# Edge keys of a windowed attention: the high and the low part of the weights on the two halves of the rows, in two products in place of four

## The chip, the cores and the metric

The kernel runs on one core of a Trainium2 chip. The metric is the device time of one execution in microseconds. A core has five engines with queues of their own: TensorE (PE in the profile, its weight loads PEld), VectorE (DVE), ScalarE (ACT), GpSimd (POOL) and SyncE (SP), which here issues most of the DMAs. Each queue is worked off in order; semaphores hold an instruction until what it reads is there.

## The reference

One layer of an encoder, applied to two requests of 2048 tokens with shared weights, all in float32. What the change touches is the first of two attentions, group A: a windowed attention with 8 query heads, 2 key-value heads and head width 64.

```python
def block(j):                                   # 128 queries, 384 keys: 128 before, the block, 128 after
    sc = jnp.einsum('bqkgd,bskd->bkgqs', qb, kb) * scale
    valid = band & ((kpos >= 0) & (kpos < s))   # |key - query| <= 128
    sc = jnp.where(valid, sc, -jnp.inf)
    m = jnp.maximum(jnp.max(sc, axis=-1, keepdims=True), sink_f)
    e = jnp.exp(sc - m)
    denom = jnp.sum(e, axis=-1, keepdims=True) + jnp.exp(sink_f - m)
    o = jnp.einsum('bkgqs,bskd->bqkgd', e / denom, vb)
...
o_a = windowed_gqa_sink(q_a, k_a, v_a, sink_a) * jax.nn.silu(g_a)
o_b = neighbourhood_attn(q_b, k_b, v_b, rpb_b) * jax.nn.silu(g_b)
x = x + jnp.concatenate([o_a, o_b], axis=-1) @ w_out
return x + (p @ w_ple) * jax.nn.sigmoid(x @ w_ple_gate)
```

Before it stand an RMS norm, one combined input projection, a norm of queries and keys and a partial rotary embedding; after it a second attention (group B) and the output layers.

## The kernel before, in words

**Two parts for each number.** TensorE multiplies in a format that keeps fewer bits than float32 (float32r). So an operand is kept as a high part (the value rounded to float32r) and a low part (the rest), and a product of two operands is a sum of products of parts. The values v of the first attention lie in a tile `vv`, rows = 128 keys, and for each key-value head 128 columns: 64 of the high part beside 64 of the low part. One product with that as the stationary operand gives both, in two halves of the rows of the result.

**Units.** The first attention goes over 32 blocks of 128 queries (`f` = 0 to 31, 16 of each request; `t` is the block in its request), each in two units, one for each key-value head (`kv`), so 64 units. A unit has 4 query heads. Its queries are split into two halves of 64, and for each half only the 320 keys that its window can reach are scored: with respect to the block, the first half needs keys -128 to 191, the second -64 to 255. Of the softmax weights, turned so that keys are rows (`pt`, line 775), there are thus three groups of rows:

- the edge keys, `pt(0)`: 64 rows. For the first half of the queries these are the first 64 keys of the next block (called right here), for the second half the last 64 keys of the block before (left). Each has 256 columns: 4 heads x 64 queries.
- `pt(1)`: 128 rows, keys of the block before for the first half of the queries and of the next for the second, 256 columns each;
- `pt(2)`: 128 rows, the block's own keys, 512 columns.

The weights come out of PSUM into three tiles `p_rot[0..2]` of 128 rows x 2 x 512 columns, which live for the whole first attention: ScalarE writes the high part (line 797, index 0 of the middle dimension), VectorE the low part (line 799, index 1). The edge keys' tile is `p_rot[0]`: the right side's weights lie in rows 0 to 63 of columns 0 to 255, the left side's in rows 64 to 127 of columns 256 to 511. The other half of the rows of each is zero, written once by two memsets of GpSimd (lines 791 and 792).

**The products.** `po(j)` (line 802) multiplies values with weights into one PSUM tile. `po(0)`: for each side that there is, two products of 256 columns, one with the high part and one with the low part of the weights, so four in an inner block and two in a block at an end of its request. The stationary operand is the neighbour block's whole value tile of 128 rows; the zeroed rows keep the other 64 keys out. `po(1)`: four products of 256 columns; `po(2)`: two of 512 columns. All products are recorded at line 287 (in `mm`), those of the weights under the name `po<-pr,vv`. `fin` (line 813) adds the two halves of the rows of the result and multiplies with the gate.

**The order of the work.** TensorE's order is written out by hand: each product is tied to the one before it (`pinned`). Between a unit's steps a stream of projection products (`pk`, `pq`, `pg`) of the block two ahead is given out by their costs, and a plan (`PLAN_A`, line 93) says at which share of the unit's stretch which step comes: (share, 1 for this unit and 0 for the one before, step, index). So scores (`sc`) of a unit stand in its own stretch, and its `pt`, `po` and `fin` in the next one's; the first head's `po(0)` thus comes in the second head's stretch at 0.48. The other engines' order comes from the compiler's scheduling, except where an instruction is tied to its place by `P` or `behind`.

**DMAs around it.** `turn` (line 749) copies a unit's softmax weights onto themselves in another format, 2 DMAs of 320 KB from SP (line 753, `tna<-s`); `pt` transposes them in the next stretch. `turn_gate` (line 366) and `turn_q` (line 740) do the same for gates and queries. Line 399 loads inputs, line 827 stores results. The projection's values are written into `vv` at lines 573 and 574, a block ahead of the block that uses them as its right neighbour.

Of the kernel before, what the change touches and what calls it, by code (L numbers as in the profile page):

```python
# [11 lines left out]
F32 = mybir.dt.float32  # L12
F32R = mybir.dt.float32r
AF = mybir.ActivationFunctionType
ALU = mybir.AluOpType
# [4 lines left out]
NT = SEQ // 128  # L20
# [38 lines left out]
def bias_offsets():  # L59
# [33 lines left out]
PLAN_A = (  # L93
    (0.04, 1, "sc", 0), (0.08, 1, "sc", 1), (0.11, 1, "sc", 2), (0.12, 1, "rest", 0), (0.14, 1, "sc", 3),
    (0.14, 1, "rest", 1), (0.21, 0, "pt", 0), (0.26, 0, "pt", 1), (0.30, 1, "qcopy", 0), (0.31, 0, "pt", 2),
    (0.32, 1, "exp", 0), (0.33, 1, "turn", 0), (0.33, 1, "turn", 1),
    (0.48, 0, "po", 0), (0.56, 0, "po", 1), (0.64, 1, "prep", 0), (0.66, 0, "po", 2), (0.67, 1, "den", 0), (0.74, 0, "fin", 0),
    (0.75, 1, "gcopy", 0),
)
# [25 lines left out]
def emit(ctx, tc, io):  # L125
    nc = tc.nc
# [4 lines left out]
    def ptile(shape, tag, name):  # L131
        tag = PSM.get(tag, tag)
        return pp.tile(shape, F32, tag=tag, name=name, bufs=PSB[tag])

    main = ctx.enter_context(tc.tile_pool(name="main", bufs=1))
# [136 lines left out]
    def pinned(ins):  # L272

        if last_pe:
            tc.add_manual_dep(ins.ins, last_pe.pop().name,
                              mybir.DependencyInfo(mybir.DependencyClass.NoSync, mybir.DependencyReason.DATA),
                              reason="tensor engine order")
        last_pe.append(ins.ins)
# [7 lines left out]
    def mm(out, lhsT, rhs, start, stop):  # L286
        pinned(nc.tensor.matmul(out, lhsT, rhs, start=start, stop=stop))  # L287
# [22 lines left out]
    def sm_tiles():  # L310
        return {"s": [], **{k: ap.tile([128, 4], F32, tag=k, name=k, bufs=3) for k in ("mx", "nm", "den", "rd")}}
# [51 lines left out]
    def turn_gate(sm):  # L363

        g2r = ap.tile([128, 256], F32R, tag="g2r", name="g2r", bufs=1)
        nc.sync.dma_start(g2r.bitcast(F32), sm["g2"])
        sm["g2"] = g2r
# [15 lines left out]
    ap = ab_stack.enter_context(tc.tile_pool(name="ab", bufs=1))  # L383
# [55 lines left out]
    def big(shape, dt, name):  # L439
        return ap.tile(shape, dt, tag="big", name=name, bufs=3)  # L440
# [69 lines left out]
    for i in range(4):  # L510
        nc.vector.tensor_tensor(out=tab[i // 2][:, i % 2], in0=cs[:, i % 2],
                                in1=rw[:, i].unsqueeze(1).broadcast_to([128, NT, 16]), op=ALU.mult)
# [7 lines left out]
    vv = big([128, NT, 2, 2, HD], F32R, "vv")  # L520
    q2s = []
    for i in range(2):
        t = ap.tile([128, 2, 512], F32R, tag=f"q2{i}", name=f"q2{i}")
# [205 lines left out]
    p_rot, s2, tn, tna, turned_q = [], [0], [], [], {}  # L729

    def turned_a():

        if not tna:
            tna.append(ap.tile([128, 1920], F32R, tag="ev", name="tna", bufs=1))
        return tna[0]

    def turn_q(f):

        turned_q[f] = turned_a()[:, 1280:1792].rearrange("p (h d) -> p h d", d=HD)
        nc.sync.dma_start(turned_q[f].bitcast(F32), held[f][0])  # L740

    def unit_a(f, kv):
        s, t = divmod(f, NT)
        _, gs, y = held[f]
        left, right = t > 0, t < NT - 1
        span = [(0 if left else 128 - 64 * half, 320 if right else 256 - 64 * half) for half in range(2)]
        sm, pairs, prs, got = sm_tiles(), [], [], {}

        def turn(pair):

            if left and right:
                to = turned_a()[:, 640 * pair:640 * pair + 640]
                nc.sync.dma_start(to.bitcast(F32), pairs[pair])
                pairs[pair] = to

        def sc(i):
            pair, half = divmod(i, 2)
            a, z = span[half]
            c0, n = 128 * t - 128 + 64 * half, z - a
            if half == 0:  # L760
                k = 640 * (s2[0] % 4)
                pairs.append(space[:, k:k + 640])
                s2[0] += 1
                if not right:
                    nc.gpsimd.memset(pairs[pair][:, 256:320], 0.0)
            ps = ptile([128, 512], "sc", "sc")
            for j, q in enumerate(qs[f]):
                mm(ps[:, :n], q[kv][:, 128 * i:128 * i + 128], ks_a[:, kv, c0 + a:c0 + z], j == 0, j == 1)
            softmax(i, ps, n, mask[:, a:z], sm, pairs[pair][:, 320 * half + a:320 * half + z])
            if i == 3:  # L770
                got["ex"] = exps(sm, y[:, 11:12], gs[:, 256 * kv:256 * kv + 256],
                                 (snk[:, 0, 4 * kv:4 * kv + 4], snk[:, 1, 4 * kv:4 * kv + 4]))
                next(got["ex"])

        def pt(j):
            pt = ptile([128, 512], "pt", "pt")
            r, c = slice(0, 128), slice(0, 512)
            if j == 0:
                r, c = slice(0 if right else 64, 128 if left else 64), slice(0, 256)
                for pair in range(2):  # L780
                    tr(pt[:r.stop, 128 * pair:128 * pair + 128], pairs[pair][:, 256:256 + r.stop])
            else:
                if j == 1:
                    c = slice(0 if left else 256, 512 if right else 256)
                for x in range(c.start // 128, c.stop // 128):
                    half, pair = divmod(x, 2)
                    col = ((0, 512), (128, 384))[j - 1][half]
                    tr(pt[:, 128 * x:128 * x + 128], pairs[pair][:, col:col + 128])
            if not p_rot:
                p_rot.extend(main.tile([128, 2, 512], F32R, tag="p_t", name="pr", bufs=3) for _ in range(3))  # L790
                nc.gpsimd.memset(p_rot[0][64:128, :, 0:256].bitcast(F32), 0.0)
                nc.gpsimd.memset(p_rot[0][0:64, :, 256:512].bitcast(F32), 0.0)
            pr = p_rot[j]
            parts = [(r, c, c)] if j else \
                [(slice(64 * x, 64 * x + 64), c, slice(256 * x, 256 * x + 256)) for x, there in enumerate((right, left)) if there]
            for r, c, to in parts:
                nc.scalar.copy(pr[r, 0, to], pt[r, c])  # L797
            for r, c, to in parts:
                nc.vector.tensor_tensor(out=pr[r, 1, to], in0=pt[r, c], in1=pr[r, 0, to].bitcast(F32), op=ALU.subtract)
            prs.append(pr)  # L800

        def po(j):
            if j == 0:
                got["po"] = ptile([128, 512], "ms", "po")
            first, second = slice(0, 256), slice(256, 512)
            steps = ([(1, first)] * right + [(-1, second)] * left, [(-1, first)] * left + [(1, second)] * right,
                     [(0, slice(0, 512))])[j]
            for d, c in steps:
                v = vv[:, t + d, kv].rearrange("p a d -> p (a d)")
                for i in range(2):  # L810
                    mm(got["po"][:, c], v, prs[j][:, i, c], j == 0 and i == 0 and d == steps[0][0], j == 2 and i == 1)

        def fin(_):
            pgt = ptile([128, 2, 128], "sc", "pgt")
            for i in range(2):
                tr(pgt[:, i, :], sm["g2"][:, 128 * i:128 * i + 128])
            ot = ap.tile([128, 2, 128], F32, tag="ot", name="ot", bufs=2)
            ph2 = got["po"].rearrange("p (x i e q) -> p e x i q", x=2, i=2, e=2)
            oh = ot.rearrange("p i (x q) -> p x i q", x=2)
            for e in range(2):  # L820
                a, z = 64 * e, 64 - 64 * e
                nc.scalar.copy(oh[a:a + 64], ph2[z:z + 64, e])
            for e in range(2):
                a = 64 * e
                nc.vector.tensor_tensor(out=oh[a:a + 64], in0=ph2[a:a + 64, e], in1=oh[a:a + 64], op=ALU.add)
            nc.vector.tensor_tensor(out=ot, in0=pgt, in1=ot, op=ALU.mult)
            nc.sync.dma_start(oa_d[s].rearrange("(i p) q -> p i q", p=128)[:, 2 * kv:2 * kv + 2, 128 * t:128 * t + 128],
                              ot)
        return {"sc": sc, "turn": turn, "gcopy": lambda _: turn_gate(sm) if f < 2 * NT - 2 else None,
                "qcopy": lambda _: turn_q(f + 1) if kv == 0 and f + 1 < 2 * NT - 2 else None, "pt": pt, "po": po, "fin": fin, "prep": lambda _: nxt(f) if kv else None,  # L830
                "exp": lambda _: next(got["ex"]), "den": lambda _: next(got["ex"]), "rest": lambda _: None if kv else next(qrest[f])}

# [345 lines left out]
    first = [filler(0), filler(1)]  # L1178
# [83 lines left out]
    with tc.tile_pool(name="c", bufs=1, reuse_waits="tile") as op:  # L1262
# [208 lines left out]
        for m in range(7 * len(groups)):  # L1471
            n, i = divmod(m, 7)
# [94 lines left out]
```

## Time and profile before

| | |
|---|---|
| median of 3 runs | 2429.82 us (2428.88 to 2432.13) |
| the profiled execution | 2431.07 us |
| its span, first to last instruction | 2429.3 us |
| granted TensorE clock, mean | 1.000 |
| product groups `po<-pr,vv` of 256 columns | 480 |
| of 512 columns | 128 |

How to read it: the profile is of one execution, a little above the median of the runs; the span leaves out what lies around the first and the last instruction. A row of a group names line, engine, operation, tile written <- tiles read, shape written <- shape read, xcount, then busy time in us, mean ns of one, and idle time of the engine just before them with what ended it. A row of the timeline has the start in us, the length in us from the first one's start to the last one's end, and how many instructions were merged (x4). TensorE's products are pipelined, so that one starts before the one ahead has ended; the step from start to start is what one takes of the queue. "idle before <- DVE pr L799" says that the engine sat idle until VectorE had written `pr` at line 799.

### The profile page before, as it was taken

The page shows a single profiled execution, that of the slowest core. Times are in us where ns is not written, and L with a number is a line of the kernel's source. Part 1 is how long each engine was busy: PE and PEld are TensorE (multiplying, and loading weights), DVE is VectorE, ACT ScalarE, POOL GpSimd, SP SyncE. Part 2 cuts the span into 40 slices and gives each one's busy share as a digit, 9 for nine tenths or more (in the row PEclk, how much of TensorE's full clock was granted, in tenths as well). Part 3 has the DMA queues.
Part 4 walks back from the last instruction along what each step waited for, and adds up shares of the span by engine and source line. Part 5 has one row for each costly group of instructions (what it writes and reads, how often), then busy time and mean ns, then how long its engine had stood idle before and what let it go on. Part 6 is the DMA issues. An engine that isn't in the chain of part 4 may idle for free.

```text
span 2429.3 us, 41554 instructions
## 1 busy us (share of the span) xinstructions
PE 2417.4 (100%) x13062; PEld 2047.4 (84%) x13062; DVE 1729.2 (71%) x4215; ACT 1427.6 (59%) x3408; POOL 848.3 (35%) x1363
## 2 busy tenths in 40 slices
PE   9999999999999999999999999999999999999999
PEld 7888888888888888888888888888888888888887
DVE  7888888888875666666666667776537665776876
ACT  6777777777764656665566666666753122344433
POOL 5555555555543544444455444443100000000000
PEclk9999999999999999999999999999999999999999
DMA  6655554555574677668876777788976545856765
GB/s 229 210 185 183 185 179 146 178 183 185 187 243 149 207 245 259 233 212 260 279 237 229 234 256 251 245 267 263 323 274 233 165 161 186 270 177 207 247 225 170
DMA packets 304204, 531.87 MB, mean 219 GB/s; under 512 B 34384, under 2 KB 126960, under 8 KB 299760
## 3 DMA queue, kind: packets, MB, share of 16 engines
q1 hardware_dynamic: 274320, 490.02, 60.3%
q10 hardware_dynamic: 29664, 39.19, 5.3%
q8 instruction: 104, 1.70, 0.3%
q14 instruction: 116, 0.95, 0.1%
HBM read 307.72 MB, written 134.23 MB: 182 GB/s over the span
## 4 chain that ended last, share of the span: by engine, by line
PE 94%; DMA 2%; ACT 1%; DVE 1%; issue 1%; POOL 0%; SPq 0%; ACTq 0%; DVEq 0%
PE pvg L287 15%; PE pqk L287 15%; PE acca L1370 14%; PE accc L1370 10%; PE pg L287 7%; PE pq L287 7%; PE scb L287 4%; PE pk L287 3%; PE po L287 3%; PE pob L287 3%; PE sc L287 3%; PE pple L287 3%; PE ptb L291 2%; PE pt L291 2%; PE ptb L293 1%
## 5 line engine op out<-in xcount | busy, mean ns | idle before, releaser
L287 PE MATMUL pvg<-wb,xr 128*128 128x512 f32 x1536 | 471.3, 408 | 0.3 <-DVE rd L354 0.3
L287 PE MATMUL pqk<-wa,xr 128*128 128x512 f32 x1536 | 432.3, 408 | 0.0
L331 ACT ACTIVATE s<-s,nm 128x320 f32<-128x320 f32 (+6 forms) x512 | 294.6, 579 | 44.3 <-DVE nm L324 30.0
L287 PEld LDWEIGHTS pvg<-wb,xr 128*128 128x128 f32 x1536 | 273.4, 189 | 33.1 <-DMA wb<-sp_1wb 0.8
L287 PEld LDWEIGHTS pqk<-wa,xr 128*128 128x128 f32 x1536 | 265.1, 188 | 38.9
L1352 ACT CAST opd<-raw 128x512 fp32r<-128x512 f32 x224 | 131.5, 618 | 269.4 <-PE acca L1370 116.6
L417 POOL TENSOR_TENSOR xr<-stx,xr 128x512 fp32r<-128x512 f32 x186 | 238.0, 1295 | 104.3 <-ACT xr L416 78.7
L1353 DVE TENSOR_TENSOR opd<-raw,opd 128x512 fp32r<-128x512 f32 x224 | 146.5, 685 | 145.4 <-ACT opd L1352 145.4
L287 PE MATMUL pq<-wa,xr 128*128 128x512 f32 x768 | 240.8, 405 | 0.0
L287 PE MATMUL pg<-wb,xr 128*128 128x512 f32 x768 | 229.5, 405 | 0.4 <-DVE vv L574 0.4
L306 DVE CUSTOM_DVE_ANT_0 s<-scb,bias 128x288 f32<-128x288 f32 (+3 forms) x256 | 139.1, 548 | 73.9 <-PE scb L287 47.2
L1052 ACT COPY otb<-pob 64x512 f32<-64x512 f32 x128 | 74.3, 581 | 182.4 <-PE pob L287 181.8
L1370 PE MATMUL accc<-opd,wb 128*128 128x512 f32 x768 | 176.7, 389 | 0.0
L1370 PE MATMUL acca<-opd,wa 128*128 128x512 f32 (+1 forms) x780 | 175.9, 386 | 0.5 <-ACT r L1448 0.5
L1370 PE MATMUL acca<-opd,s 128*128 128x512 f32 x768 | 175.4, 389 | 0.0
L1370 PEld LDWEIGHTS acca<-opd,wa 128*128 128x128 f32 x780 | 145.0, 188 | 30.2 <-ACT r L1448 0.7
L1370 PEld LDWEIGHTS accc<-opd,wb 128*128 128x128 f32 x768 | 144.2, 188 | 29.9
L1370 PEld LDWEIGHTS acca<-opd,s 128*128 128x128 f32 x768 | 144.2, 188 | 29.9
L170 POOL TENSOR_TENSOR yb<-vrb,power 128x8 f32<-128x8 f32 x64 | 106.2, 1659 | 152.3 <-DVE vrb L872 134.6
L287 PEld LDWEIGHTS pg<-wb,xr 128*128 128x128 f32 x768 | 135.7, 188 | 16.8 <-DVE vv L574 0.8
L797 ACT CAST pr<-pt 128x512 fp32r<-128x512 f32 (+2 forms) x248 | 112.1, 474 | 54.3 <-PE pt L291 47.3
L287 PEld LDWEIGHTS pq<-wa,xr 128*128 128x128 f32 x768 | 132.7, 189 | 11.3
(196 smaller groups left out, 5143.3 us busy)
## 6 DMA issues: line engine op xcount, KB each, us to landing
tna<-s SPq DMA_DIRECT2D x112, 320.0 KB
stx<-x_b SPq DMA_DIRECT2D x128, 256.0 KB
vw<-v_d SPq DMA_DIRECT2D x96, 256.0 KB
v_d<-vb SPq DMA_DIRECT2D x64, 256.0 KB
xres<-x_r SPq DMA_DIRECT2D x64, 256.0 KB
raw<-x_d SPq DMA_DIRECT2D x16, 1024.0 KB
xres<-ple_d SPq DMA_DIRECT2D x64, 256.0 KB
xres<-x_d SPq DMA_DIRECT2D x64, 256.0 KB
```

The lines of the kernel that those rows point to most:

```text
L170: nc.gpsimd.tensor_tensor(out=y, in0=v, in1=power.broadcast_to([128, n]), op=ALU.pow)
L287: pinned(nc.tensor.matmul(out, lhsT, rhs, start=start, stop=stop))
L291: pinned(nc.tensor.transpose(out.bitcast(F32R), in_, eye))
L293: pinned(nc.tensor.transpose(out, in_, eye.bitcast(F32)))
L306: nc.vector.tensor_tensor_reduce(out=s, in0=ps[:, :n], in1=bias, scale=1.0, scalar=-3.0e38, op0=ALU.add, op1=ALU.max, accum_out=sm["mx"][: ...
L331: ex = nc.scalar.activation(ss[i], ss[i], AF.Exp, bias=nm[:, i:i + 1], accum_out=den[:, i:i + 1])
L417: low.tensor_tensor(out=lo, in0=raw, in1=hi.bitcast(F32), op=ALU.subtract)
L797: nc.scalar.copy(pr[r, 0, to], pt[r, c])
L1052: nc.scalar.copy(ot[a:a + 64], pq[z:z + 64])
L1352: P(nc.scalar.copy(hi, v))
L1353: P(nc.vector.tensor_tensor(out=lo, in0=v, in1=hi.bitcast(F32), op=ALU.subtract))
L1370: pinned(nc.tensor.matmul(ps[:, cols], w[k][:, a, c:c + 128], o[:, b, cols], start=i in (0, 1, 4) and k == 0 and j == 0, stop=k == 3 and j ...
```

## The change

The edge keys' low part no longer goes to a place of its own but into the half of the rows that was zero: for the right side the high part in rows 0 to 63 and the low part in rows 64 to 127, for the left side the other way round. The stationary operand becomes a tile that holds the 64 edge keys' values twice, on rows 0 to 63 and on rows 64 to 127, so that one product of 256 columns sums over both parts. `po(0)` has two products in an inner block instead of four, one instead of two at an end.

The doubled values are copied by DMA from `vv`, in a new step `twice` at 0.44 of the first head's stretch, for both heads at once (256 columns): two DMAs for each side, one for each half of the rows. There are two sets of buffers, used by turns of `f`: one side's in the now unused low half of `p_rot[0]`, the other's in two new tiles under the tag `o_t` of the second attention. The memsets go, and `p_rot` is made by `take_p`, which the first `twice` may call before the first `pt`.

```diff
-    (0.32, 1, "exp", 0), (0.33, 1, "turn", 0), (0.33, 1, "turn", 1),
+    (0.32, 1, "exp", 0), (0.33, 1, "turn", 0), (0.33, 1, "turn", 1), (0.44, 1, "twice", 0),
...
+    twice = []
+
+    def take_p():
+
+        p_rot.extend(main.tile([128, 2, 512], F32R, tag="p_t", name="pr", bufs=3) for _ in range(3))
+
+    def edge_values(f):
+
+        s, t = divmod(f, NT)
+        if not p_rot:
+            take_p()
+        if not twice:
+            twice.extend((p_rot[0][:, 1, 256 * i:256 * i + 256], ap.tile([128, 256], F32R, tag="o_t", name="twice", bufs=2))
+                         for i in range(2))
+        for to, d, a, there in zip(twice[f % 2], (1, -1), (0, 64), (t < NT - 1, t > 0)):
+            for e in range(2) if there else ():
+                nc.sync.dma_start(to[64 * e:64 * e + 64].bitcast(F32),
+                                  vv[a:a + 64, t + d].bitcast(F32).rearrange("p k a d -> p (k a d)"))
...
-                p_rot.extend(main.tile([128, 2, 512], F32R, tag="p_t", name="pr", bufs=3) for _ in range(3))
-                nc.gpsimd.memset(p_rot[0][64:128, :, 0:256].bitcast(F32), 0.0)
-                nc.gpsimd.memset(p_rot[0][0:64, :, 256:512].bitcast(F32), 0.0)
+                take_p()
             pr = p_rot[j]
-            parts = [(r, c, c)] if j else \
-                [(slice(64 * x, 64 * x + 64), c, slice(256 * x, 256 * x + 256)) for x, there in enumerate((right, left)) if there]
-            for r, c, to in parts:
-                nc.scalar.copy(pr[r, 0, to], pt[r, c])
-            for r, c, to in parts:
-                nc.vector.tensor_tensor(out=pr[r, 1, to], in0=pt[r, c], in1=pr[r, 0, to].bitcast(F32), op=ALU.subtract)
+            if j:
+                nc.scalar.copy(pr[r, 0, c], pt[r, c])
+                nc.vector.tensor_tensor(out=pr[r, 1, c], in0=pt[r, c], in1=pr[r, 0, c].bitcast(F32), op=ALU.subtract)
+            else:
+                parts = [(slice(64 * x, 64 * x + 64), slice(64 - 64 * x, 128 - 64 * x), slice(256 * x, 256 * x + 256))
+                         for x, there in enumerate((right, left)) if there]
+                for r, z, to in parts:
+                    nc.scalar.copy(pr[r, 0, to], pt[r, c])
+                for r, z, to in parts:
+                    nc.vector.tensor_tensor(out=pr[z, 0, to], in0=pt[r, c], in1=pr[r, 0, to].bitcast(F32), op=ALU.subtract)
...
-            steps = ([(1, first)] * right + [(-1, second)] * left, [(-1, first)] * left + [(1, second)] * right,
-                     [(0, slice(0, 512))])[j]
+            if j == 0:
+                edges = [(0, first)] * right + [(1, second)] * left
+                for d, c in edges:
+                    mm(got["po"][:, c], twice[f % 2][d][:, 128 * kv:128 * kv + 128], prs[0][:, 0, c], d == edges[0][0], False)
+                return
+            steps = ([(-1, first)] * left + [(1, second)] * right, [(0, slice(0, 512))])[j - 1]
...
-        return {"sc": sc, "turn": turn, "gcopy": lambda _: turn_gate(sm) if f < 2 * NT - 2 else None,
+        return {"sc": sc, "turn": turn, "twice": lambda _: None if kv else edge_values(f), "gcopy": lambda _: turn_gate(sm) if f < 2 * NT - 2 else None,
```

More of the change, by code (lines that the diff above doesn't have):

```diff
@@ L810, in po @@
                 for i in range(2):
-                    mm(got["po"][:, c], v, prs[j][:, i, c], j == 0 and i == 0 and d == steps[0][0], j == 2 and i == 1)
+                    mm(got["po"][:, c], v, prs[j][:, i, c], False, j == 2 and i == 1)
         def fin(_):
```

## The prediction

> **What bounds the kernel now.** I read the page's summary, its chain of work that ended last, then the busy times by stretches, then TensorE's groups by shape, and last the timeline of one block of the first attention.
>
> ```profile
> span 2429.3 us, 41554 instructions
> ...
> PE 2417.4 (100%) x13062; PEld 2047.4 (84%) x13062; DVE 1729.2 (71%) x4215; ACT 1427.6 (59%) x3408; POOL 848.3 (35%) x1363
> ...
> PE 94%; DMA 2%; ACT 1%; DVE 1%; issue 1%; POOL 0%; SPq 0%; ACTq 0%; DVEq 0%
> ```
>
> TensorE (PE) is busy for all but 12 us, and the chain runs over it. The first attention's value products run from 53 to 743 us:
>
> ```profile
> L287 PE MATMUL po<-pr,vv x608: 273/282/505, 53.2 to 742.7; 128*128 128x256 f32 x120, 128*128 128x512 f32 x32
> ```
>
> (That row samples the shapes; the full counts come below.) In these two stretches of it the columns are length, then busy PE, weight loads, Vector, Scalar, Pool with instruction counts, then granted clock, DMA share and GB/s:
>
> ```profile
> 53.00:660.00 607.00, 606.75 (x3813) 536.42 (x3812) 504.74 (x1510) 460.58 (x1254) 333.07 (x707) 1.00 0.54 180
> 660.00:743.00 83.00, 81.82 (x450) 67.40 (x450) 61.37 (x169) 54.41 (x145) 38.81 (x75) 1.00 0.64 218
> ```
>
> PE has no idle time there to 660 us, at the full granted clock 1.00; Vector follows with 504.74 of 607, 83%. So a product that goes should shorten the span by its place in PE's queue, as long as Vector's results are there earlier too. The group that the change touches, over the first attention:
>
> ```profile
> L287 PE MATMUL po<-pr,vv 128*128 128x256 f32 x480 | 78.4, 281 | 0.4 <-DVE pr L799 0.2
> ```
>
> The 480 are four edge and four other 256-column products in full blocks. 32 blocks have 64 sides, four sides at the ends of the two sequences don't exist, so 60 sides, times 2 key-value heads, times 2 edge and 2 other products. The change halves the edge ones: 120 products go. The mean of 281 ns is not their price, because products overlap; the price is the step from one start to the next. One full block, both heads (the group at 303.37 is a second head's, that at 314.07 a first head's):
>
> ```profile
> 303.37 0.64 PE L287 MATMUL po<-pr,vv 128*128 128x256 f32 x4
> 303.84 0.63 PE L287 MATMUL pq<-wa,xr 128*128 128x512 f32 x2
> 304.31 0.63 PE L287 MATMUL po<-pr,vv 128*128 128x256 f32 x4
> 304.78 0.85 PE L287 MATMUL pq<-wa,xr 128*128 128x512 f32 x3
> 305.46 0.62 PE L287 MATMUL po<-pr,vv 128*128 128x512 f32 x2
> ...
> 311.31 0.29 PE L291 MATMUL pt<-ident,tna 128*128 128x128 f32 x2
> ...
> 314.07 0.64 PE L287 MATMUL po<-pr,vv 128*128 128x256 f32 x4
> 314.55 0.86 PE L287 MATMUL pg<-wb,xr 128*128 128x512 f32 x3
> 315.25 0.63 PE L287 MATMUL po<-pr,vv 128*128 128x256 f32 x4
> ```
>
> Four edge products take 303.84 - 303.37 = 0.47 us, 0.118 each; at 314.07 they take 0.48.
>
> **The change part by part.** *The products.* 120 x 0.118 = 14.1 us leave PE's queue, 0.235 in each of 56 full head-units (14 inner blocks x 2 requests x 2 heads) and 0.118 in the eight at the sequence ends. They lie on the path, since PE doesn't idle there. All else follows from whether the next work is ready 0.235 us sooner.
>
> *Who must be earlier.* Before, the four products read, in order, the high part of one side, its low part, the high part of the other side, its low part. Now the first reads both parts of one side, the second both parts of the other. The second side's low part is due at the second product, 0.12 us after the group's start, where it was due at the fourth, 0.35 after. Vector makes the low parts:
>
> ```profile
> 301.93 0.23 DVE L589 TENSOR_SCALAR vr<-ssq,ee 128x2 f32<-128x2 f32 x1
> 302.19 0.88 DVE L799 TENSOR_TENSOR pr<-pt,pr 64x256 fp32r<-64x256 f32 x2
> 303.10 0.16 DVE L345 TENSOR_TENSOR es<-snk,nm 128x4 f32<-128x4 f32 x1
> 303.29 0.69 DVE L799 TENSOR_TENSOR pr<-pt,pr 128x512 fp32r<-128x512 f32 x1
> 303.90 0.68 DVE L660 SCALAR_TENSOR_TENSOR gs<-gs,pg 128x512 f32<-128x512 f32 x1
> 304.49 0.69 DVE L799 TENSOR_TENSOR pr<-pt,pr 128x512 fp32r<-128x512 f32 x1
> ...
> 312.52 0.69 DVE L630 TENSOR_TENSOR q<-pq,y 128x512 f32<-128x512 f32 x1
> 313.12 2.18 DVE L799 TENSOR_TENSOR pr<-pt,pr 64x256 fp32r<-64x256 f32 x4
> ```
>
> How early must a low part end? A unit in which Vector was late shows it:
>
> ```profile
> 550.70 2.18 DVE L799 TENSOR_TENSOR pr<-pt,pr 64x256 fp32r<-64x256 f32 x4
> 551.21 0.79 PE L287 MATMUL po<-pr,vv 128*128 128x256 f32 x4
> 551.84 0.86 PE L287 MATMUL pg<-wb,xr 128*128 128x512 f32 x3
> ...
> 715.71 0.94 PE L287 MATMUL po<-pr,vv 128*128 128x256 f32 x4
> 716.48 0.62 PE L287 MATMUL pvg<-wb,xr 128*128 128x512 f32 x2
> ```
>
> The pair of low parts (0.88 as above) ends at 551.58, and the product behind the fourth starts at 551.84, 0.26 later instead of 0.12. So a low part that sets the pace has to end 0.14 us ahead of its product's turn. With that: at 303.37 the pair ends at 302.19 + 0.88 = 303.07 and is due at 303.49 - 0.14 = 303.35; cover 0.28. At 314.07 the pair ends at 314.00, due at 314.19 - 0.14 = 314.05; cover 0.05. The later products of the second head come 0.235 sooner: the low part that ends at 303.98 is due at the second product of its group, 304.31 - 0.235 + 0.12 - 0.14 = 304.06, cover 0.08; that which ends at 304.49 + 0.69 = 305.18 at the second 512-column product, one step of 0.23 in, 305.46 - 0.235 + 0.23 - 0.14 = 305.32, cover 0.14. All four covers hold, narrowly, so nothing there takes the gain back by itself.
>
> *The other half of the rows.* The low part now is written 64 rows away from where it is read. Two groups bound the duration of that: L545 reads one half and writes the other, L926 stays on its half.
>
> ```profile
> L926 DVE SCALAR_TENSOR_TENSOR q<-pqtb,wk,q1b 64x256 fp32r<-64x256 f32 x128 | 61.4, 479 | 10.6 <-ACT q1b L925 8.2
> L545 DVE SCALAR_TENSOR_TENSOR ks_a<-pkt,wk,ks_a 64x128 fp32r<-64x128 f32 x64 | 22.4, 350 | 3.0 <-ACT ks_a L542 1.5
> ```
>
> 128 columns less are 129 ns less; that is 1.0 ns a column, as between the 128x512 and the 64x256 form of L799 ((0.69 - 0.42) / 256). So the distance costs nothing in duration. Its start may differ: 303.90 begins 0.08 before 303.29 + 0.69 is over, 313.12 begins 0.09 before 312.52 + 0.69 is, but the two halves' pair needs 0.88 for 2 x 0.42, so the change of rows waits for the end and 0.03 more. No row shows an instruction that changes only the rows of its output. The bounds are 0 and 0.12 us; I take 0.12, the nearest row being the pair. At 302.19 nothing overlaps in front (301.93 + 0.23 is over by then), so nothing is lost there. At 313.12 the pair then ends at 314.12, 0.07 late: 28 first-head units x 0.07 = 2.0 us. With 0 instead, this term is 0.
>
> [...]
>
> *Units that Vector already delays.* In the groups at 551.21 and 715.71 the low part's end sets the end of the group (0.63 and 0.77 instead of 0.47), so two products fewer gain nothing there: 2 x 0.235 = 0.5 us off the gain.
>
> *The copies.* Each side of each block now needs two copies of 64 rows x 1 KB = 64 KB: 120 in all, 7.9 MB, over 690 us 11 GB/s beside 180; the DMA share would go from 0.54 to about 0.57. They queue on SP behind the turned weights (tna) of the first head:
>
> ```profile
> 304.07 1.55 SPq L753 DMA_DIRECT2D tna<-s  x2
> 308.13 0.47 SPq L366 DMA_DIRECT2D g2r<-g  x1
> ```
>
> With 0.47 each, four take 1.9 us, and SP issues nothing between 305.62 and 308.13. Their sources were written by a projection that was over before this block began, and the buffers that they overwrite were last read two blocks back, so I expect no wait in them. Queued behind them is L366, whose gates are transposed a unit later. The first product now waits for two landings, with all of PE's queue behind it. A bound on landing: the turned weights, ten times the bytes, are issued until 305.62 and read at 311.31 without PE waiting, so they take under 5.7 us; copies issued by 307.6 are read at 314.07, 6.5 us later. Whatever holds them up holds up the turned weights, which are read earlier, first. Cost taken: 0, below nothing is excluded since nothing is taken off these queues; if the cover went, each microsecond of lateness would come back once for each of 30 blocks. Pool's two memsets at the start go; Pool is 0% of the chain. ACT's instructions stay as they are.
>
> **Sum.** 14.1 - 2.0 - 0.5 = 11.6 us less. The profiled execution took 2431.07 us (its span and 1.8 around it), so 2419.5; it stands 1.25 above the median of 2429.82, from which the forecast is 2429.82 - 11.6 = 2418.2.
>
> **The rivals.** *Paid back as waits.* The covers of 0.05 to 0.14 are not enough, and each full unit gives its 0.235 back: 56 x 0.235 = 13.2 of 14.1, leaving 2428.9, no measurable change. For it: Vector is 83% busy and nearly without gaps around 303. Against it: it has 17% left, and its queue gets no longer. [...] Chance 0.10.
>
> *Slower: Vector's queue in another order.* That order is fixed when the program is compiled, and the low parts aren't tied to a place in it as PE's products are. If one 128x512 operation (step 303.90 - 303.29 = 0.61) lands ahead of the pair in every full unit, the first head's second product is 0.07 + 0.61 = 0.68 late, the second head's 0.61 - 0.28 = 0.33: 1.01 x 28 = 28.3, less 13.6 (14.1 and the 0.5), gives 2444.5. It decides from a pair that ends 0.35 later in both heads (0.42 + 0.07 per block, about the 0.47 gained). For it: at 550.70 the pair is 0.44 later than in the other first-head units. Against it: that is one unit in the whole stretch. Chance 0.06.
>
> *Copies in the way.* If they are put ahead of the turned weights and wait there, those are late once the hold passes the cover of less than 5.7 us; 1 us beyond it is 30 us, 2448. Nothing that they wait for is that late. Chance 0.04.
>
> **How the numbers follow.** The forecast's case has 0.80; it is faster. A measurement of this kernel tells a difference from about 0.2%, 4.9 us. Rival one is the case of no change, 0.10; the other two are slower, 0.10. Low end of the range: 14.1 in full, the 1.2 us of PE idle in the second stretch gone too, and the runs' spread of 0.9 below their median: 2413.5. High end: the late unit's price of 0.16 (0.63 - 0.47) in all 28 first-head units, 4.5, and the runs' spread of 2.3 above: 2425. The rivals lie outside.
>
> **What would show it.** Right: 360 products in the 128x256 group; edge groups of two that take 0.235; the first attention over about 11 us sooner and nothing changed behind it; 120 copies of 64 KB, and PE never waiting for one; the first low part of a first head starting after L630's end. Wrong: gaps or long steps in front of the second edge product or of the 512-column products (rival one), another order of L799 among its neighbours (two), PE or the turned weights waiting for DMA (three).

## The result, and the profile after

| | before | after |
|---|---|---|
| median, on one chip | 2432.92 us (15 runs, 2428.88 to 2435.47) | 2424.61 us (15 runs, 2422.05 to 2428.03) |
| ratio after / before | | 0.9966 [0.9958, 0.9974] |
| the profiled execution | 2431.07 us | 2423.36 us |
| its span | 2429.3 us | 2421.3 us |

The change makes the kernel faster by 8.3 us (6.3 to 10.2 by the interval); 11.6 was forecast. The time lies inside the range, near its upper end; counted from the kernel before on the same chip, 2432.92 - 11.6 = 2421.3 would have been right, and 3.3 us are missing. The page of the changed kernel, its summary and its chain:

```profile
span 2421.3 us, 41534 instructions
...
PE 2408.6 (99%) x12942; PEld 2033.6 (84%) x12942; DVE 1729.9 (71%) x4215; ACT 1427.4 (59%) x3408; POOL 849.1 (35%) x1361
...
PE 95%; DMA 2%; DVE 1%; ACT 1%; issue 0%; POOL 0%; SPq 0%; DVEq 0%; ACTq 0%
```

120 matmuls fewer (13062 to 12942), Vector's work the same, and the chain still runs over TensorE. The product groups of the first attention by shape, window 50 to 745 us:

```profile
L287 PE MATMUL po<-pr,vv 128*128 128x256 f32 x240 | 39.3, 282 | 0.2 <-DVE pr L813 0.2
L287 PE MATMUL po<-pr,twice 128*128 128x256 f32 x60 | 19.0, 317 | 0.8 <-DVE pr L820 0.7
L287 PE MATMUL po<-pr 128*128 128x256 f32 x60 | 17.0, 283 | 0.1
```

480 have become 240 + 60 + 60 = 360. `po<-pr` are the right side's edge products, whose doubled values lie in `p_rot[0]` itself, `po<-pr,twice` the left side's, the second of a group. Only these have idle time of note ahead of them, and a longer mean (317 ns against 283). Line 820 writes the edge keys' low part now, line 813 the others'. The block shown before, in the timeline of the changed kernel, TensorE first:

```profile
300.31 0.28 PE L287 MATMUL po<-pr 128*128 128x256 f32 x1
300.43 0.28 PE L287 MATMUL po<-pr,twice 128*128 128x256 f32 x1
300.55 0.63 PE L287 MATMUL pq<-wa,xr 128*128 128x512 f32 x2
...
310.83 0.28 PE L287 MATMUL po<-pr 128*128 128x256 f32 x1
310.96 0.36 PE L287 MATMUL po<-pr,twice 128*128 128x256 f32 x1
311.15 0.85 PE L287 MATMUL pg<-wb,xr 128*128 128x512 f32 x3
```

The second head's group takes 300.55 - 300.31 = 0.24, as forecast. The first head's takes 311.15 - 310.83 = 0.32. Vector's timeline of the same block says why:

```profile
299.16 0.87 DVE L820 TENSOR_TENSOR pr<-pt,pr 64x256 fp32r<-64x256 f32 x2
...
309.26 0.69 DVE L630 TENSOR_TENSOR q<-pq,y 128x512 f32<-128x512 f32 x1
309.98 0.87 DVE L820 TENSOR_TENSOR pr<-pt,pr 64x256 fp32r<-64x256 f32 x2
310.89 1.29 DVE L813 TENSOR_TENSOR pr<-pt,pr 128x512 fp32r<-128x512 f32 x2
```

L630 is over at 309.95; the low parts start 0.03 behind that, where before they started 0.09 ahead of it. They end at 310.85, only 0.11 ahead of the second product's start, and that product is late. What TensorE waited for in the first attention (total us, times, longest; 50 to 745 us):

```profile
PE pgt L291 <- DMA g2r<-g: 1.3, 1, 1.3
PE po L287 <- DVE pr L820: 0.7, 2, 0.6
```

The first row is new and has nothing to do with the edge products: once, near the end, TensorE waits for a block's gates. No row names the copies.

Where the gain arises is read from the starts of the 64 groups of edge products. The table has the start before, and how much earlier (-) or later (+) the same point comes in each kernel's profile; "again" is a second profile of the same kernel. Groups 10 to 30 are ten inner blocks with nothing but the steady pattern.

| | before, us | after | after again | before again |
|---|---|---|---|---|
| group 0 | 53.21 | +0.68 | +0.86 | +0.02 |
| group 10 | 161.34 | -0.85 | -0.67 | +0.04 |
| group 30 | 379.19 | -4.25 | -4.11 | +0.05 |
| group 59 | 696.86 | -8.43 | -8.45 | +0.04 |
| group 63, the last | 738.80 | -7.23 | -8.07 | +0.16 |
| span | 2429.27 | -7.99 | -5.64 | +0.84 |

A block gains (4.25 - 0.85) / 10 = 0.34 us, 0.34 again in the second profile; 0.40 had been forecast (0.47 less 0.07). The table shows two more losses: about 0.7 before the first group, and the last groups, which give 0.4 to 1.2 back. Behind the first attention the two profiles of one and the same kernel differ by some 1 to 3 us, so nothing is read from single differences there.

### The profile page after: what moved, and what is told of

It reads as the page before. It is cut to its first block, busy times and chain, and to the rows that moved or that the text cites. A ratio compares the mean times of both kernels' runs of the same rounds, so it can differ in the third digit from the quotient of the medians.

```text
span 2421.3 us, 41534 instructions
## 1 busy us (share of the span) xinstructions
PE 2408.6 (99%) x12942; PEld 2033.6 (84%) x12942; DVE 1729.9 (71%) x4215; ACT 1427.4 (59%) x3408; POOL 849.1 (35%) x1361
## 4 chain that ended last, share of the span: by engine, by line
PE 95%; DMA 2%; DVE 1%; ACT 1%; issue 0%; POOL 0%; SPq 0%; DVEq 0%; ACTq 0%
PE pvg L287 15%; PE pqk L287 15%; PE acca L1395 14%; PE accc L1395 10%; PE pq L287 7%; PE pg L287 7%; PE pk L287 4%; PE scb L287 4%; PE pob L287 3%; PE pple L287 3%; PE po L287 3%; PE sc L287 3%; PE ptb L291 2%; PE pt L291 2%; PE ptb L293 1%; PE pktb L293 1%
## 5 line engine op out<-in xcount | busy, mean ns | idle before, releaser
L287 PEld LDWEIGHTS pq<-wa,xr 128*128 128x128 f32 x768 | 132.4, 188 | 11.3
L306 DVE CUSTOM_DVE_ANT_0 s<-sc,mask 128x320 f32<-128x320 f32 (+2 forms) x256 | 121.5, 478 | 20.4 <-PE sc L287 11.9
```

The source lines that it names most:

```text
L306: nc.vector.tensor_tensor_reduce(out=s, in0=ps[:, :n], in1=bias, scale=1.0, scalar=-3.0e38, op0=ALU.add, op1=ALU.max, accum_out=sm["mx"][: ...
```

## The experiments

My theory after the result: two products fewer are worth what was forecast; the low part written to other rows costs more than was forecast; the rest goes in a DMA wait at the end. Rivals: the copies disturb something; or the products themselves are worth less. The times below are medians of 5 to 11 runs beside the kernel before on the same chip, whose median was 2431.70 us (17 runs) for the first four and 2431.93 us (15 runs) for the next four.

**The products alone.** The kernel before; of the edge keys only the low-part products are left, without copies and without a change of rows.

```diff
-                for i in range(2):
+                for i in range(2) if j else (1,):
...
```

> The kernel before, with the two edge products that read the high part left out, so two products read the low part from its old place; the edge keys' high part is left out of the result. No copies, no write to the other half of the rows, the low parts due at the first and the second product as in the change. Theory (the queue's 0.118 us a product, with small terms lost to Vector's low part in the first head's units and to the weight loads at the end of the first attention): the groups of both heads are 0.23 to 0.24 shorter, 0.47 a block, and the whole is 11.5 to 13 us faster than before, more than the change by 3 to 4. Rival (the copies take nothing and the other half of the rows takes nothing, the products are worth less than their step): 0.35 a block as in the change, 8 us.

Measured: 2421.70 us, ratio 0.9956 [0.9944, 0.9969]: 10.0 us less, where 11.5 to 13 was expected. From group 10 to 30 it gains 4.44, 0.44 a block. Followed product by product, each full edge group is shorter by 0.24 (from 0.475 to 0.235) and the second product waits for nothing; of the 0.48 a block so gained 0.04 trickles back in steps of mostly under 0.015 between the other products, which I did not follow up. So the first term stands, less 0.03 a block against the 0.47 forecast. It too waits 1.1 us for the gates near the end, with no copy in it.

**Without the copies.** The changed kernel, the products reading `vv` directly.

```diff
-    (0.33, 1, "turn", 1), (0.44, 1, "twice", 0),
+    (0.33, 1, "turn", 1),
...
-  mm(got["po"][:, c], twice[f % 2][d][:, 128 * kv:128 * kv + 128], prs[0][:, 0, c], ...)
+  mm(got["po"][:, c], vv[:, t + 1 - 2 * d, kv].rearrange("p a d -> p (a d)"), prs[0][:, 0, c], ...)
```

> The changed kernel without its copies: the two edge products read the neighbour's whole value tile in place of the doubled one, so the result of the edge keys is wrong. Theory (the copies are hidden; what was lost is the first head's low part, started later because it goes to the other half of the rows, and the gates that wait behind the weight loads at 690 us): the first head's group still takes 0.32 instead of 0.235, the wait of 1.3 us for the gates is still there, and the time is that of the change within 1.5 us. Rival (the copies delay the gates and other DMAs): the wait at 690 us goes, and with the drift of some 0.05 a block the kernel is 2.5 to 3 us faster than the change.

Measured: 2424.95 us, 0.9973 [0.9963, 0.9984], no faster than with them. The block gains 0.31, and the gates are waited for again (0.9 us). The first head's group takes 0.38 on average, not the 0.32 expected; why it is longer than with the copies was not followed up. The copies take nothing from the gain.

**The low part on its own rows.** The changed kernel, the low part written over the high part, so that Vector's output does not change rows; two memsets clear the other half.

```diff
+        nc.gpsimd.memset(p_rot[0][64:128, 0, 0:256].bitcast(F32), 0.0)
+        nc.gpsimd.memset(p_rot[0][0:64, 0, 256:512].bitcast(F32), 0.0)
...
-  nc.vector.tensor_tensor(out=pr[z, 0, to], in0=pt[r, c], in1=pr[r, 0, to].bitcast(F32), op=ALU.subtract)
+  nc.vector.tensor_tensor(out=pr[r, 0, to], in0=pt[r, c], in1=pr[r, 0, to].bitcast(F32), op=ALU.subtract)
```

> The changed kernel, with the low part written over the high part on the rows where it was read, the other half zero: no write to the other half, the same copies, products and waits; the high part is left out of the edge products. Theory (a Vector instruction that changes the rows of its output alone starts only after the one ahead has ended, 0.12 us later): the first head's low parts start about 0.1 before the end of the instruction ahead again, its group of two takes 0.235 instead of 0.32, and the whole is 2 us faster than the change. Rival (the 0.08 comes from the new due time alone, not from the rows): the group still takes 0.32, and the time is that of the change.

Measured: 2422.53 us, 0.9958 [0.9945, 0.9970]. Vector's and TensorE's timelines of the first head's group, in two fences:

```profile
308.05 0.69 DVE L630 TENSOR_TENSOR q<-pq,y 128x512 f32<-128x512 f32 x1
308.66 0.86 DVE L822 TENSOR_TENSOR pr<-pt,pr 64x256 fp32r<-64x256 f32 x2
```

```profile
309.63 0.28 PE L287 MATMUL po<-pr 128*128 128x256 f32 x1
309.75 0.28 PE L287 MATMUL po<-pr,twice 128*128 128x256 f32 x1
309.87 0.87 PE L287 MATMUL pg<-wb,xr 128*128 128x512 f32 x3
```

The low parts start 0.08 before L630 is over (308.05 + 0.69 = 308.74), and the group takes 0.24 again. The block gains 0.43. So the rows of the output, and nothing else of the change, cost 0.09 a block: from group 10 to 30 this kernel gains 4.34 where the change gains 3.40. The median is 9.2 us under before's, 0.9 more than the change's 8.3 and not the 2 expected; the two intervals overlap, so the reading rests on the blocks.

**The copies alone**, in the kernel before, into tiles that nobody reads.

```diff
-    (0.33, 1, "turn", 1),
+    (0.33, 1, "turn", 1), (0.44, 1, "twice", 0),
```

> The kernel before, with the change's copies into two tiles of their own that nothing reads, at the same place of the plan; all four edge products stay. Theory (the copies are hidden): the time of before within 1 us, and no wait for the gates at the end of the first attention. Rival (the copies delay other DMAs): 1.5 to 3 us slower than before, with PE waiting for gates or turned weights.

Measured: 2433.13 us, 1.0006 [0.9997, 1.0016]. From group 10 to group 30 the difference stays at 0.73: 0.00 a block. But near the end:

```profile
PE pgt L291 <- DMA g2r<-g: 1.6, 1, 1.6
```

No such wait was expected here; the rival had one. It doesn't need the earlier arrival of TensorE, then. Nor does it need the copies: the kernels without them wait too (above 1.1 and 0.9 us, below 0.8). The time, 1.4 us more than before's, is not told apart from it by the interval.

**The other rows alone.** The kernel before with four products; only the place that the low part is written to changes (and two memsets more).

```diff
-                nc.vector.tensor_tensor(out=pr[r, 1, to], in0=pt[r, c], ...)
+                nc.vector.tensor_tensor(out=pr[z, 1, to], in0=pt[r, c], ...)
```

> The kernel before, all four edge products and no copies, with the low part alone written to the other half of the rows (so it meets the other 64 keys' values and the low part of the edge keys is wrong). The low part of the second side is due only at the fourth product. Theory (a Vector instruction whose output alone changes rows starts after the end of the one ahead): in the first head's units the first low part starts 0.03 after the end of the operation ahead in place of 0.09 before it, the pair ends 0.12 later, no product waits, and the time is that of before within 1 us. Rival (only the change of input rows holds it): the first low part still starts 0.09 before that end.

Measured: 2433.71 us, 1.0007 [0.9998, 1.0016], 0.00 a block (0.41 later at group 10, 0.43 at group 30); it too waits for the gates, 0.8 us. The median is 1.8 us over before's, where under 1 was expected; the interval includes no difference. Vector's timeline, first head:

```profile
312.93 0.69 DVE L630 TENSOR_TENSOR q<-pq,y 128x512 f32<-128x512 f32 x1
313.65 2.19 DVE L802 TENSOR_TENSOR pr<-pt,pr 64x256 fp32r<-64x256 f32 x4
```

313.65 is 0.03 behind the end of L630 at 313.62. Only the rows of the output differ from the kernel before, so that is the hold by itself: 0.09 + 0.03 = 0.12. It costs nothing here, because with four products the second side's low part is due 0.23 later. What is paid is the part of the hold that the cover doesn't hide: 0.09 of 0.12 in the changed kernel, nothing here.

**A later place for the products.** The changed kernel, the first edge product moved from share 0.48 to 0.51 of the stretch; one more 512-column product stands ahead of it (six in place of five).

```diff
-    (0.48, 0, "po", 0), (0.56, 0, "po", 1),
+    (0.51, 0, "po", 0), (0.56, 0, "po", 1),
```

> The changed kernel with the first edge step at 0.51 of the stretch in place of 0.48, which puts one more 512-column product (0.23 us) ahead of it. Theory (the first head's group loses 0.1 a block because its second product comes before the low part that Vector starts 0.12 later): the group takes 0.235 again, the block gains 0.43 to 0.44 on the kernel before in place of 0.34, and the whole is 2.5 us faster than the change. Rival (the loss sits elsewhere on Vector's chain): the low parts of the later groups become late instead, and the block still gains 0.34.

Measured: 2421.41 us, 0.9956 [0.9943, 0.9968]. Vector's rows, then TensorE's:

```profile
307.89 0.69 DVE L630 TENSOR_TENSOR q<-pq,y 128x512 f32<-128x512 f32 x1
308.62 0.88 DVE L820 TENSOR_TENSOR pr<-pt,pr 64x256 fp32r<-64x256 f32 x2
```

```profile
308.24 1.62 PE L287 MATMUL pg<-wb,xr 128*128 128x512 f32 x6
309.70 0.28 PE L287 MATMUL po<-pr 128*128 128x256 f32 x1
309.81 0.28 PE L287 MATMUL po<-pr,twice 128*128 128x256 f32 x1
309.93 0.62 PE L287 MATMUL pg<-wb,xr 128*128 128x512 f32 x2
```

The hold is still there (308.62 against 308.58), but the pair ends at 309.50, 0.31 before the second product, and the group takes 0.23. The block gains 0.44, all that the products can give, and the median is 10.5 us under before's, 2.2 more than the change's 8.3 (2.5 was expected).

**The gates of block 29.** The changed kernel; that block's gates are not copied by DMA but turned as they are.

```diff
-  "gcopy": lambda _: turn_gate(sm) if f < 2 * NT - 2 else None,
+  "gcopy": lambda _: turn_gate(sm) if f < 2 * NT - 3 else None,
```

> The changed kernel in which the gates of block 29 are not copied by DMA before they are transposed (as those of blocks 30 and 31 already are not), so TensorE doesn't wait for that copy behind the weight loads. Theory (the wait of 1.3 us at the end of the first attention is the price of a DMA that queues behind 8 MB of weights and was hidden by 0.5 us before): the step of 1.3 there is gone, and the kernel is 1.0 to 1.3 us faster than the change. Rival (TensorE, now ahead of the weights, waits for the next DMA instead): the loss moves to the next unit, and the time stays within 0.3 us of the change.

Measured: 2424.29 us, 0.9968 [0.9955, 0.9980], as the change itself. No wait for gates is left, but from group 59 to 63 the kernel still loses 0.98 (the change: 1.20 and, again, 0.38). The waits from 670 to 745 us:

```profile
PE po L287 <- DVE pr L820: 1.3, 3, 0.6
```

Without the gates' wait TensorE comes to these units earlier, and Vector's low parts are late instead: in the changed kernel this row has 0.7. So the theory failed, and the rival is nearer (7.6 us under before's, the change 8.3), but what TensorE waits for next is Vector, not a DMA.

**Both.** The two edits together.

> Both edits: the first edge step at 0.51 and block 29's gates without the copy. Theory: the gains add up, 3.5 us faster than the change, 11.5 to 12 faster than before. Rival (either loss comes back at another place): under 2 us faster than the change.

Measured: 2420.65 us, 0.9954 [0.9941, 0.9966], the lowest median of all. It is 11.3 us under before's, 3.0 more than the change's 8.3. From group 59 to 63 it loses 0.52. TensorE still waits for low parts twice there, 0.7 us in all; the longer wait is this:

```profile
695.05 0.39 PE L287 MATMUL po<-pr 128*128 128x256 f32 x1 [0.40 <-DVE pr L820]
```

It is faster than the kernel before by 8 to 14 us. That it also beats the changed kernel is likely but not certain from these times: 0.9954 against 0.9966, measured at another time, with intervals that overlap. Between groups 0 and 59, where the two profiles of the changed kernel agree to 0.2 (9.1 and 9.3 gained), it gains 0.21 + 11.61 = 11.8, and the kernel with the later place alone 0.77 + 11.18 = 12.0.

**Both kernels profiled again**, unchanged.

> The kernel before, unchanged, profiled a second time, to see which differences between two profiles come from the execution and not from an edit. One theory: the products of the first 10 us, the wait for the gates of block 29 at the end of the first attention (none in the first profile of before, 1.6 us with the copies alone, 0.8 us with the other rows alone) and one to two us in the second attention vary from execution to execution. Then this profile is behind the first one by 0.4 to 0.9 us at the first group of the first attention, not at all over the groups from 10 to 30, and waits 0 to 1.6 us for the gates. The other theory: the wait for the gates belongs to the edits alone; then there is none here and the first attention ends within 0.5 us of the first profile's end.

> The changed kernel, unchanged, profiled a second time, for the same purpose. If the gain of a block is the kernel's, it is 0.34 again over the groups from 10 to 30 (3.4 us in 10 blocks) against either profile of before. If the wait for the gates is a matter of the execution, it is anywhere from 0 to 1.6 us here; if it comes with the earlier arrival of TensorE, it is 1.1 to 1.5 again.

Measured: spans of 2430.1 and 2423.6 us; the table above has the points. Of the two theories for the kernel before the first failed and the other held: its second profile repeats the first to 0.06 up to group 59, has no wait for the gates, and is 0.84 longer only behind the first attention. The changed kernel waits for the gates again, but a third as long:

```profile
PE pgt L291 <- DMA g2r<-g: 0.4, 1, 0.4
```

So the wait has come in every edited kernel that copies these gates, and in neither profile of before. Its size differs between executions of one and the same kernel (1.3 and 0.4); over all of them it is 0.4 to 1.6.

## Why the prediction was right or wrong

**The direction, right.** TensorE had no holes up to 660 us (busy for 606.75 of 607), so products that go shorten the span, and none of the three rivals came. Not "paid back as waits": of 0.47 a block 0.34 stays, and 0.44 in the kernel with the later place. Not "Vector's queue in another order": L820 keeps its place behind L630 and ahead of L345 or the other low parts. Not "copies in the way": no wait of TensorE names them, and alone they cost 0.00 a block. Their place in SP's queue was not the forecast's, though: the first of them stands between the turned weights, not behind them, as these rows of the changed kernel show.

```profile
301.04 0.47 SPq L772 DMA_DIRECT2D tna<-s  x1
301.91 0.48 SPq L758 DMA_DIRECT2D twice<-vv  x1
302.48 0.54 SPq L772 DMA_DIRECT2D tna<-s  x1
```

So the second half of the turned weights is issued 1.44 behind the first, where it was 1.08 before (304.07 + 1.55 - 0.47 = 305.15); their cover took the 0.36. (The prediction's bound for the landing says "ten times the bytes"; the turned weights' 640 KB are ten times one copy, but two and a half times the four.)

**The products: 0.235 a full unit, right.** 0.24 measured by themselves. Not counted was the 0.04 a block that trickles back behind them; 0.44 a block is left of the 0.47 forecast.

**The low part on the other rows: the mechanism right, the size too small.** Between the bounds 0 and 0.12 the prediction took 0.12, by the nearest row, the pair; the start 0.03 behind L630's end was forecast, and measured. The kernel with the other rows alone shows the same: with nothing but the output's rows changed, the pair starts 0.03 behind the end (313.65 against 313.62) in place of 0.09 before it (313.12 against 313.21 in the kernel before). "28 first-head units x 0.07 = 2.0 us" is 0.094 in the runs ((4.34 - 3.40) / 10), 2.6 in all: the product behind the second started 311.15 - 310.85 = 0.30 after the pair's end, and the prediction had 0.26 from the group at 551.21, whose rows show the fourth of four products.

**The units that Vector delays.** The prediction took 0.235 for the group at 551.21. From group 45 to group 47 (540.50 and 562.48 before) it goes from -6.49 to -6.30 in the changed kernel, 0.19 lost, where the forecast had a gain of 0.235 - 0.07 = 0.17: 0.4 more. TensorE's and Vector's rows of the late group, changed kernel:

```profile
543.67 1.09 PE L287 MATMUL pg<-wb,xr 128*128 128x512 f32 x4
544.84 0.39 PE L287 MATMUL po<-pr 128*128 128x256 f32 x1
545.34 0.36 PE L287 MATMUL po<-pr,twice 128*128 128x256 f32 x1
545.54 0.63 PE L287 MATMUL pg<-wb,xr 128*128 128x512 f32 x2
```

```profile
543.64 0.69 DVE L630 TENSOR_TENSOR q<-pq,y 128x512 f32<-128x512 f32 x1 [0.64 <-POOL y L170]
544.37 0.88 DVE L820 TENSOR_TENSOR pr<-pt,pr 64x256 fp32r<-64x256 f32 x2
```

L630 waits for Pool here, and the pair ends at 545.25. Four products of 0.23 would let the first edge product start at 543.67 + 0.92 = 544.59; it starts at 544.84, 0.05 after the first of the pair ends (544.37 + 0.42): it, too, now reads a low part, where before it read a high one. The second is late on top, and the group takes 0.70 where four products took 0.63. The prediction had this unit gain nothing; it loses.

**"The first attention over about 11 us sooner and nothing changed behind it": the step that failed.** Its own terms up to group 59 are 53 x 0.235 + 6 x 0.118 - 27 x 0.07 - 0.235 = 11.0; the profiles gave 9.1 and 9.3. The three points above account for it: a block gained 0.34 in place of 0.40, over 27 blocks 1.6, and the late unit lost 0.4; that is 2.0, where 1.7 to 1.9 is missing. Of the 0.06 a block, 0.03 are the products' and 0.02 the low part's; 0.01 I can't place. Then two things were missing from the sum.

*At the end*, groups 59 to 63 should have gained another 0.5 (0.235 + 0.165 + 0 + 0.118) and lost 1.2 (and 0.4 when profiled again). The largest part is the wait for the gates of block 29. The issue and the read, before:

```profile
693.83 0.52 SPq L366 DMA_DIRECT2D g2r<-g  x1
```

```profile
699.73 0.34 PE L291 MATMUL pgt<-ident,g2r 128*128 128x128 f32 x2
```

and after:

```profile
680.16 3.08 SPq L224 DMA_DIRECT2D wb<-sp_0wb  x5
...
686.22 0.52 SPq L366 DMA_DIRECT2D g2r<-g  x1
```

```profile
692.69 0.34 PE L291 MATMUL pgt<-ident,g2r 128*128 128x128 f32 x2 [1.30 <-DMA g2r<-g]
```

Before, TensorE reads 5.9 us after the issue and doesn't wait. After, it is there 5.2 us after the issue (692.69 - 1.30 - 686.22) and waits until 6.5. What the gates are queued with shows in the stretch from the issue on (columns as in the prediction):

```profile
687.00:693.00 6.00, 4.70 (x27) 3.57 (x26) 4.71 (x12) 4.35 (x14) 1.89 (x6) 1.00 1.04 370
```

The DMA engines are full, at a share of 1.04: loads of 512 KB each of the next stage's weights (L224) had been issued until 683.24, and the gates' 128 KB take 6.5 us behind them. But they were as full before (1.02), where such loads had been issued until 691.83:

```profile
694.00:700.00 6.00, 6.00 (x39) 5.02 (x39) 5.24 (x18) 4.69 (x15) 2.06 (x4) 1.00 1.02 365
```

So the loads alone don't make the wait. What differs is little: the issue comes 0.7 us closer to TensorE's arrival (5.2 us ahead of it in place of 5.9), and the transfer takes 6.5 us, where before it took at most 5.9. In the changed kernel the issue had itself stood in SP's queue until one of these loads had landed (SP's waits from 680 to 696 us):

```profile
SPq L366 <- DMA wb<-sp_0wb: 0.9, 1, 0.9
```

In six of the profiles with the wait the transfer took about 6.2 to 7.0 us and TensorE came about 4.9 to 6.2 us after the issue; in the first of before it came after 5.9 and found the gates there; no row shows how long they had been there. Why the transfer is that long in the edited kernels isn't shown, so the cause of this wait stays open. That TensorE comes 8 us sooner is not the reason by itself: the loads came sooner too, and the copies alone bring the wait. The prediction named the gates' copy as queued behind its own copies, but worked out a cover only for the copies and the turned weights. And taken away, the wait is followed by Vector's lateness in the same units, for about as much.

*At the start*, the changed kernel reaches its first group 0.7 to 0.9 later; 0 was forecast. The stretch from 8 to 11 us (columns as above) before, after, and in the kernel with both edits, which change nothing of this stretch:

```profile
8.00:11.00 3.00, 3.00 (x22) 2.82 (x22) 3.00 (x8) 2.39 (x7) 0.00 (x0) 1.00 1.03 395
```

```profile
8.00:11.00 3.00, 3.00 (x15) 3.00 (x15) 2.85 (x8) 2.41 (x7) 0.00 (x0) 1.00 1.03 391
```

```profile
8.00:11.00 3.00, 3.00 (x23) 2.82 (x23) 3.00 (x8) 2.41 (x6) 0.00 (x0) 1.00 1.04 391
```

15 products where there are 22 and 23, without idle time. So the changed kernel's start can be as fast as before's. In its own first profile these products step at 0.213 us (see the last section), and its second has 15 of them in the stretch again; why stays open.

**Sum.** The forecast was 11.6. The profile has -0.7 at the start, 9.1 in place of 11.0 to group 59, -1.2 in place of 0.5 to the last group, and 0.8 gained behind it, which is within what repeats differ by there: 8.0. The second profile has -0.9, 9.3, -0.4 and 2.4 lost behind the first attention, so only the middle part is steady. The medians give 8.3. The forecast was 3.3 too high on the same chip, and that the time still lies inside the range owes something to its high end: 2418.2 + 4.5 + 2.3 = 2425 charges the first-head units 4.5 on top of the 2.0 that the forecast already takes for them. Charged once, it is 2423.0, and 2424.61 lies above that; it is inside only when the range is counted from the kernel before on the same chip (2432.92, where the prediction had 2429.82).

## What to carry to other kernels

When two instructions become one, the one is due when the first was: ask of each of its inputs how much earlier that is. A producer's output that moves to other rows may start 0.12 us later even if it does the same work; that is free with cover, and without it most of it is paid (0.09 here); moving the consumer back by one product of other work (a change of a single share in the plan) buys the cover. And look at small transfers that queue with a burst of large loads: one that is just in time before can be late after any edit, even after one that gains nothing, so its slack belongs in the sum.

## What the runs showed of the hardware

- Behind L630, Vector's first low part starts 0.03 to 0.04 us after the end of L630 when its output lies 64 rows further than its inputs (309.98 against 309.95 in the changed kernel, 313.65 against 313.62 with the other rows alone, 308.62 against 308.58 with the later place), and 0.08 to 0.09 before that end when it doesn't (308.66 against 308.74 with the low part on its own rows, 313.12 against 313.21 in the kernel before); nothing else of the instruction differs.
- In the changed kernel's first profile the 256-column products that start from 8.06 to 9.55 us step at 0.213 (1.49 over seven steps; 15 products in the 3.00 us from 8 to 11), at a granted clock of 1.00 in the view. The kernel before has 22 in the same 3.00 us, also at 1.00. From 11.3 to 12.2 us both step at 0.12. What makes the difference was not shown.
- 128 KB issued behind 512 KB loads were there 6.5 us later, at 370 GB/s and a DMA share of 1.04; at 365 GB/s and 1.02, before, they were there within 5.9 us.
